# RMSNorm and matmul on one core: without four reads of 12 to 15 rows on the SyncE queue

## Chip, core and metric

The kernel runs on 1 core of one Trainium2 chip. The metric is the device time of one execution in microseconds (us). Engines are named as in the profile: PE is TensorE (matmul), PEld its weight load, DVE is VectorE, ACT is ScalarE, POOL is GpSimd and SP is SyncE, which here only issues DMAs. A name with a q (SPq) is the sequencer of that engine. L191 is line 191 of the kernel.

## What is computed

```python
# x: [16, 1024, 512] float32, gamma: [512], weight: [512, 768], eps = 1e-5
rms = np.sqrt(np.mean(x ** 2, axis=-1, keepdims=True) + eps)
x_norm = x / rms * gamma
return np.matmul(x_norm, weight).astype(np.float32)
```

The 16 x 1024 rows are flattened to 16,384 rows of 512. The output has 16,384 rows of 768.

## The kernel before

**Tiles.** The rows are cut into NT = 128 tiles of 128 rows, and the main loop runs over NP = 64 pairs of tiles; j is the pair. x comes in by groups of 16 tiles (XG), in two buffers `xt`, most groups as two loads of 8 tiles (2 MB each). The output leaves by groups of 8 tiles (OG), in three buffers `ot`: one store of 3 MB for a group, and smaller stores for the first two groups and the last. The last group is stored as two halves of 4 tiles (1.5 MB each).

**Work on a pair.** POOL casts x to bf16 (`cast`, L94; `cast_quad`, L158). For most pairs PE transposes it, two bf16 values taken as one float32 word (`transpose_word`, L133), and DVE copies the result out of PSUM (`evac`, L140). From the second group on, the last two pairs of each group of 16 tiles are transposed by DVE in 32x32 blocks instead (L172). ACT computes the sum of squares (`square`, L98) and the root (L102), and DVE the reciprocal (L104). PE multiplies by the weights (`matmul`, L194), which have been scaled by gamma and cast to bf16 once. `finish_tile` scales the accumulator by 1/rms into `ot`, on ACT (L176) for the first tile of a pair and on DVE (L178) for the second, and calls `store`, which issues a DMA (L191) when the last tile of its stretch is done.

**Order.** The order on each engine is that in which the code is written; there is no scheduler. All loads of x, the weights and all stores are issued on SP, so they stand in one queue there. `load_until` issues the loads ahead of use; the last two are issued in the pass of j = 47. From then on SP issues only stores, and the four reads below. A DMA also waits for the previous user of its completion semaphore; eight of these are used in rotation by the DMAs of SP and ACT.

**The reads.** `probe` is a buffer of 16 partitions and 16 x 64 floats, which nothing reads. `mark` issues for each k in its list one DMA on SP (L265), from the first 4k floats of the first k rows of x, to k partitions of `probe`. `marks` calls it once, at j = NP - 10 = 54, with k = 12, 13, 14, 15. Each of the k rows is a packet of 16k bytes: 192, 208, 224 and 240 bytes.

Of the kernel before, what the change touches and what calls it, by code (L numbers as in the profile page):

```python
# [12 lines left out]
F32 = mybir.dt.float32  # L13
# [5 lines left out]
def kernel(  # L19
# [8 lines left out]
    nc = tc.nc  # L28
    P = 128

    x = x.flatten_outer_dims()
    out = out.flatten_outer_dims()
# [4 lines left out]
    NP = NT // 2  # L37
# [25 lines left out]
    singles = ctx.enter_context(tc.tile_pool(name="singles", bufs=1))  # L63
# [23 lines left out]
    def load_until(i):  # L87
        while starts and starts[0] < i:
            load(starts.pop(0))

    def cast(i, engine, n=1):
        if i // 2 not in xb_tiles:
            xb_tiles[i // 2] = xbp.tile([P, 2, D], BF16, name="xb")
        engine.tensor_copy(out=xb_tiles[i // 2][:, i % 2:i % 2 + n, :], in_=held(x_tiles, XG, i, n))  # L94
# [13 lines left out]
    def norms(i, n):  # L108
        ssq = stats.tile([P, 4], F32, name="ssq")
        for t in range(n):  # L110
            square(i + t, ssq[:, t:t + 1])
        root(i, n, ssq)
# [30 lines left out]
    def transpose_tile(i):  # L143
        for h in range(2):
            transpose_word(i // 2, i % 2, h)
        evac(i // 2, i % 2, 1)
# [6 lines left out]
    def quad_of(j):  # L153
        return j // 2 if (2 * j) % XG >= XG - 4 and 2 * j >= XG else None

    def cast_quad(q):
        quads[q] = quad_in.tile([P, 4, D], BF16, name="xq")
        nc.gpsimd.tensor_copy(out=quads[q], in_=held(x_tiles, XG, 4 * q, 4))  # L158
        turned = quad_out.tile([P, 4, 2, P, 2], BF16, name="xTq")
        for n in range(2):  # L160
            xT_tiles[2 * q + n] = turned[:, 2 * n:2 * n + 2]
        words = quads.pop(q).rearrange("p t d -> p (t d)").bitcast(F32).rearrange("p (a w) -> p a w", w=P)
        out_words = turned.rearrange("p t h m c -> p (t h m c)").bitcast(F32).rearrange("p (a m) -> p a m", m=P)
        for tokens in range(0, P, B):
            for features in range(0, P, B):
                quad_moves.append((out_words[features:features + B, :, tokens:tokens + B],
                                   words[tokens:tokens + B, :, features:features + B]))

    def move_quad(n):
        for _ in range(min(n, len(quad_moves))):  # L170
            dst, src = quad_moves.pop(0)
            nc.vector.transpose(out=dst, in_=src)  # L172

    def scale(engine, dst, src, r):
        if engine is nc.scalar:
            nc.scalar.mul(out=dst, in_=src, mul=r)  # L176
        else:
            nc.vector.tensor_single_scalar(out=dst, in_=src, scalar=r, op=mybir.AluOpType.mult)  # L178

    def accumulator():  # L180
        return opsum.tile([P, 2, WIDE], F32, name="ops").rearrange("p a b -> p (a b)")
# [16 lines left out]
    def matmuls(i, acc, ks, feed=None):  # L198
        for k in ks:
            matmul(i, k, acc, 0, WIDE)  # L200
            if feed:
                feed()
            matmul(i, k, acc, WIDE, O)

    def finish_tile(i, acc, engine):
        scale(engine, out_tile(i), acc[:, :O], rstd_of[i])
        store(i)


    def feeder(pairs, gaps, alone=False):  # L210
        queue = [(j, t, h) for j in pairs for t in range(2) for h in range(2)]
        calls = iter(gaps)

        def feed():
            for _ in range(next(calls)):
                j, t, h = queue.pop(0)
                transpose_word(j, t, h)
                if alone and h == 1:
                    evac(j, t, 1)
                elif (t, h) == (1, 1):  # L220
                    evac(j)
        return feed

    with tc.manual_schedule():
        g_row = singles.tile([2, P, 2], F32)
        nc.scalar.dma_start(out=g_row, in_=gamma.rearrange("(h w c) -> h w c", w=P, c=2))
        nc.scalar.preload_act_table(AF.Sqrt)  # L227
        wv = weight.rearrange("(h w c) o -> w h (c o)", w=P, c=2)
        w_f32 = singles.tile([P, K, O], F32)

        def load_weights(h):
            nc.sync.dma_start(out=w_f32[:, 2 * h:2 * h + 2, :].rearrange("p c o -> p (c o)"), in_=wv[:, h, :])  # L232

        load_until(2)
        load_weights(0)
        load_weights(1)
        load_until(2 * XG)

        for _ in range(20):
            nc.sync.drain()  # L240


        warm = singles.tile([P, WIDE], BF16)
        nc.vector.memset(warm, 0.0)
        eps_sb = singles.tile([P, 1], F32)
        nc.vector.memset(eps_sb, float(eps))  # L246
        ident_f = singles.tile([P, P], F32)
        make_identity(nc, ident_f)
        spare = accumulator()

        def warm_up(n):
            for _ in range(n):
                nc.tensor.matmul(out=spare[:, :WIDE], lhsT=warm[:, :P], rhs=warm, start=True, stop=True)  # L253

        w_bf = singles.tile([P, K, O], BF16)

        def weights(k, engine, lo=0, hi=O):
            scale(engine, w_bf[:, k, lo:hi], w_f32[:, k, lo:hi], g_sb[:, k % 2, k // 2:k // 2 + 1])


        probe = singles.tile([16, 16 * 64], F32)

        def mark(counts):
            for k in counts:
                nc.sync.dma_start(out=probe[:k, 64 * k:64 * k + 4 * k], in_=x[:k, :4 * k])  # L265

        warm_up(6)
        gp = tpsum.tile([P, 2, 2], F32, name="tp")
        for c in range(2):
            nc.tensor.transpose(out=gp[:, c, :], in_=g_row[:, :, c], identity=ident_f[:2, :2])  # L270
        g_sb = singles.tile([P, 2, 2], F32)
        nc.vector.tensor_copy(out=g_sb, in_=gp)  # L272
        cast(0, nc.gpsimd)
        cast(1, nc.gpsimd)
        cast(2, nc.gpsimd, 2)
        norms(0, 2)
        warm_up(4)
        transpose_tile(0)
        transpose_tile(1)
        warm_up(2)  # L280
        weights(0, nc.vector, 0, WIDE)
        weights(0, nc.vector, WIDE, O)
        weights(1, nc.scalar)
        acc = [accumulator() for _ in range(2)]
        for i in range(2):
            matmuls(i, acc[i], [0, 1])
        weights(2, nc.vector)
        weights(3, nc.scalar)
        norms(2, 2)
        cast(4, nc.gpsimd)  # L290
        cast(5, nc.gpsimd)
        matmuls(0, acc[0], [2, 3])
        finish_tile(0, acc[0], nc.scalar)
        matmuls(1, acc[1], [2, 3], feeder([1], [2, 2], alone=True))
        finish_tile(1, acc[1], nc.vector)
        cast(6, nc.gpsimd, 2)

        mid, one, two, both = ([0, 0, 1, 1, 0, 1, 1, 0], [1, 1, 0, 1, 1, 0, 0, 0], [1, 0, 1, 0, 1, 0, 1, 0],
                               [1, 1, 1, 1, 1, 1, 1, 1])
        marks = {NP - 10: (12, 13, 14, 15)}  # L300
        for j in range(1, NP):
            load_until((2 * j + AHEAD + XG - 1) // XG * XG)
            if j + 3 < NP and quad_of(j + 3) is None:
                cast(2 * j + 6, nc.gpsimd, 2)
            if (2 * j + 2) % XG == 0 and 2 * j + 2 < NT:
                cast_quad((2 * j + 2 + XG - 4) // 4)
            elif 2 * j >= XG:
                move_quad(3)
            if j < 4:
                norms(2 * j + 2, 2)  # L310
            if 3 <= j < NP - 2:
                norms_by_four(j + 2)
            if j in marks:
                mark(marks[j])
            if j < 3:
                feed = feeder([j + 1], mid if j == 1 else one, alone=j == 1)
            elif j == 3:
                feed = feeder([4, 5], both)
            elif j + 2 < NP and quad_of(j + 2) is None:
                feed = feeder([j + 2], two)  # L320
            else:
                feed = None
            for i, engine in ((2 * j, nc.scalar), (2 * j + 1, nc.vector)):
                a = accumulator()
                matmuls(i, a, range(K), feed)
                finish_tile(i, a, engine)
# [35 lines left out]
```

## Time and profile before

| what | value |
|---|---|
| median of 6 runs | 210.61 us (210.40 to 210.86) |
| the profiled execution, its own time | 210.46 us |
| its span, first to last instruction | 208.7 us |
| mean granted TensorE clock | 0.979 |
| read from HBM, written to it | 35.14 MB, 50.33 MB |
| mean DMA rate over the span | 411 GB/s |
| busy share of PE, DVE, ACT, POOL | 93%, 72%, 72%, 31% |
| DMA issues | 1 on ACT, 42 on SP |

The issues on SP are 16 loads of x, 2 of the weights, 20 stores and the 4 reads. "Busy" is the time in which an engine works on instructions; issuing and waiting do not count. The DMA share is the mean busy share of the core's 16 DMA engines; 1.00 means that all 16 are at work (single stretches can read slightly above it, since a packet counts where it begins). Landing times come from the semaphore updates that a DMA makes, one for each of the DMA engines that carry a part of it.

### The profile page before, as it was taken

The numbers are of one execution on the slowest core, as the hardware profiler recorded it, in microseconds if no ns is written. First come the engines' busy times: TensorE is split into PE (matmuls) and PEld (weight loads), VectorE is DVE, ScalarE is ACT, GpSimd is POOL, SyncE is SP. The second block draws the span as 40 slices with busy tenths as digits, with TensorE's granted clock in tenths as the row PEclk, the third lists the DMA queues.
The fourth block names the chain that finished last, engine by engine and source line by source line (L and its number), as shares of the span: only waits on it lengthen the run. The fifth ranks groups of instructions, "written<-read, shape, count | busy, mean of one in ns | idle before, by whom it ended". The sixth has DMA issues, their size and how long they took to land.

```text
span 208.7 us, 3478 instructions
## 1 busy us (share of the span) xinstructions
PE 194.3 (93%) x1238; PEld 129.6 (62%) x1238; DVE 150.9 (72%) x270; ACT 149.3 (72%) x358; POOL 64.6 (31%) x65
## 2 busy tenths in 40 slices
PE   7799999999999999999999999999999999999700
PEld 2367767665667666666766667666676667766400
DVE  0465657997399957998499957998499957998300
ACT  4698787778677887788777887788777884986300
POOL 3247535003910292055210562006610365000000
PEclk9999999999999999999999999999999999999965
DMA  6999999999999999999999999999999999999991
GB/s 241 425 440 433 345 409 419 473 422 405 448 438 419 430 410 429 427 443 435 418 418 440 437 429 415 421 438 433 440 421 413 440 435 443 420 396 400 388 415 75
DMA packets 5601, 85.69 MB, mean 411 GB/s; under 512 B 718, under 2 KB 720, under 8 KB 1488
## 3 DMA queue, kind: packets, MB, share of 16 engines
q1 hardware_dynamic: 5580, 85.47, 96.9%
q8 instruction: 9, 0.15, 0.3%
q14 instruction: 8, 0.07, 0.1%
q10 hardware_dynamic: 4, 0.00, 0.0%
HBM read 35.14 MB, written 50.33 MB: 410 GB/s over the span
## 4 chain that ended last, share of the span: by engine, by line
PE 78%; DMA 14%; POOL 1%; DVE 1%; SPq 1%; issue 1%; POOLq 0%
PE ops L194 69%; DMA xt<-in_x_dram 14%; PE tp L133 9%; POOL xb L94 1%; DVE ot L178 1%; SPq L232 0%; SPq L83 0%; SPq L191 0%; POOLq L94 0%; DVE xT L140 0%
## 5 line engine op out<-in xcount | busy, mean ns | idle before, releaser
L194 PE MATMUL ops<-w_bf,xT 128*128 128x512 bf16 (+1 forms) x800 | 147.5, 326 | 0.6 <-DVE w_bf L178 0.6
L194 PEld LDWEIGHTS <-xT 128*128 128x128 bf16 x800 | 78.3, 98 | 46.3 <-issue 0.8
L176 ACT ACTIVATE ot<-ops,rstd 128x768 f32<-128x768 f32 x64 | 57.6, 901 | 41.9 <-PE ops L194 39.5
L94 POOL CAST xb<-xt 128x1024 bf16<-128x1024 f32 (+1 forms) x52 | 51.1, 1010 | 97.6 <-DMA xt<-in_x_dram 86.2
L98 ACT ACTIVATE jk<-xt 128x512 bf16<-128x512 f32 x128 | 78.8, 619 | 1.9 <-DMA xt<-in_x_dram 1.9
L178 DVE TENSOR_SCALAR ot<-ops,rstd 128x768 f32<-128x768 f32 x64 | 64.6, 1010 | 9.5 <-PE ops L194 9.0
L133 PE MATMUL tp<-ident_f,xb 128*128 128x128 f32 x200 | 53.9, 273 | 1.1 <-POOL xb L94 1.1
L140 DVE COPY xT<-tp 128x1024 bf16<-128x1024 bf16 (+1 forms) x53 | 34.7, 656 | 25.3 <-PE tp L133 24.5
L172 DVE STREAM_TRANSPOSE xTq<-xq 32x256 f32<-32x256 f32 x112 | 48.7, 435 | 1.9
L194 PE MATMUL ops<-w_bf,xTq 128*128 128x512 bf16 x224 | 42.8, 326 | 0.0
L133 PEld LDWEIGHTS tp<-ident_f,xb 128*128 128x128 f32 x200 | 28.1, 141 | 4.9 <-POOL xb L94 2.4
L194 PEld LDWEIGHTS <-xTq 128*128 128x128 bf16 x224 | 22.0, 98 | 12.3
L98 ACT ACTIVATION_READ_ACCUMULATOR jk<-xt 128x1 f32 x128 | 24.4, 190 | 0.0
L158 POOL CAST xq<-xt 128x2048 bf16<-128x2048 f32 x7 | 13.3, 1896 | 12.6 <-DMA xt<-in_x_dram 8.8
L102 ACT ACTIVATE rms<-ssq,eps_sb 128x4 f32<-128x4 f32 (+1 forms) x35 | 10.4, 297 | 1.1
L104 DVE RECIPROCAL rstd<-rms 128x4 f32<-128x4 f32 (+1 forms) x35 | 6.1, 175 | 6.1 <-ACT rms L102 5.4
L253 PE MATMUL ops<-warm 128*128 128x512 bf16 x12 | 5.0, 571 | 1.2 <-DVE eps_sb L246 1.2
L253 PEld LDWEIGHTS <-warm 128*128 128x128 bf16 x12 | 1.4, 128 | 2.9 <-issue 1.7
L176 ACT ACTIVATE w_bf<-w_f,g_sb 128x768 bf16<-128x768 f32 x2 | 1.9, 936 | 1.3 <-DMA w_f<-in_weight_dram 1.3
L272 DVE COPY g_sb<-tp 128x4 f32<-128x4 f32 x1 | 0.2, 163 | 3.2 <-PE tp L270 3.2
L227 ACT ACT_TABLE_LOAD x1 | 1.3, 1283 | 1.3 <-PEq L343 1.3
L178 DVE TENSOR_SCALAR w_bf<-w_f,g_sb 128x512 bf16<-128x512 f32 (+2 forms) x3 | 1.4, 482 | 0.5 <-DMA w_f<-in_weight_dram 0.5
(10 smaller groups left out, 1.9 us busy)
## 6 DMA issues: line engine op xcount, KB each, us to landing
out_dram<-ot SPq DMA_DIRECT2D x13, 3072.0 KB, 18.0
xt<-in_x_dram SPq DMA_DIRECT2D x11, 2048.0 KB, 18.3
xt<-in_x_dram SPq DMA_DIRECT2D x2, 4096.0 KB
out_dram<-ot SPq DMA_DIRECT2D x5, 1536.0 KB, 10.9
w_f<-in_weight_dram SPq DMA_DIRECT2D x2, 768.0 KB, 4.9
out_dram<-ot SPq DMA_DIRECT2D x2, 768.0 KB, 17.8
xt<-in_x_dram SPq DMA_DIRECT2D x2, 512.0 KB, 3.4
xt<-in_x_dram SPq DMA_DIRECT2D x1, 1024.0 KB
```

The source lines that it names most:

```text
L94: engine.tensor_copy(out=xb_tiles[i // 2][:, i % 2:i % 2 + n, :], in_=held(x_tiles, XG, i, n))
L98: nc.scalar.activation(out=jk, in_=held(x_tiles, XG, i)[:, 0, :], func=AF.Square, accum_out=ssq)
L102: nc.scalar.activation(out=rms[:, :n], in_=ssq[:, :n], func=AF.Sqrt, scale=1.0 / D, bias=eps_sb)
L104: nc.vector.reciprocal(out=rstd[:, :n], in_=rms[:, :n])
L133: nc.tensor.transpose(out=tp_tiles[j][:, t, h, :], in_=words[:, lo:lo + P], identity=ident_f)
L140: nc.vector.tensor_copy(out=dst[:, t:t + n, :], in_=src[:, t:t + n, :])
L158: nc.gpsimd.tensor_copy(out=quads[q], in_=held(x_tiles, XG, 4 * q, 4))
L172: nc.vector.transpose(out=dst, in_=src)
L176: nc.scalar.mul(out=dst, in_=src, mul=r)
L178: nc.vector.tensor_single_scalar(out=dst, in_=src, scalar=r, op=mybir.AluOpType.mult)
L194: nc.tensor.matmul(out=acc[:, lo:hi], lhsT=xT_tiles[i // 2][:, i % 2, k // 2, :, k % 2], rhs=w_bf[:, k, lo:hi], start=(k == 0), stop=(k == ...
L253: nc.tensor.matmul(out=spare[:, :WIDE], lhsT=warm[:, :P], rhs=warm, start=True, stop=True)
```

## The change

The buffer `probe`, the function `mark`, the dictionary `marks` and the call are removed. Nothing else differs. In the built program SP has 102 instructions in place of 106, and the other engines have the same instructions in the same order. The last four stores use other completion semaphores of the rotation, and the buffers that are allocated behind `probe` may lie elsewhere in SBUF.

```diff
-        probe = singles.tile([16, 16 * 64], F32)
-
-        def mark(counts):
-            for k in counts:
-                nc.sync.dma_start(out=probe[:k, 64 * k:64 * k + 4 * k], in_=x[:k, :4 * k])
...
-        marks = {NP - 10: (12, 13, 14, 15)}
         for j in range(1, NP):
             load_until((2 * j + AHEAD + XG - 1) // XG * XG)
...
-            if j in marks:
-                mark(marks[j])
```

## Prediction

> **What bounds the kernel now.** I read the page first, then the end of the run by stretches, then SP's waits and SP's timeline, then the line of the four reads, and last the trace's records of single packets and semaphore updates around them.
>
> The page, sections 1 and 3 (busy us, share, instructions; then queue, packets, MB, share of 16 engines):
>
> ```profile
> span 208.7 us, 3478 instructions
> ...
> PE 194.3 (93%) x1238; PEld 129.6 (62%) x1238; DVE 150.9 (72%) x270; ACT 149.3 (72%) x358; POOL 64.6 (31%) x65
> ...
> q1 hardware_dynamic: 5580, 85.47, 96.9%
> q8 instruction: 9, 0.15, 0.3%
> q14 instruction: 8, 0.07, 0.1%
> ```
>
> TensorE is busy for 93% of the span, but the 16 DMA engines are busy for 97%. Two things are near their limit, and the end must tell which one sets the time. The end by stretches (us, then busy time and count of each engine, granted clock, DMA share, GB/s):
>
> ```profile
> 160.00:187.00 27.00, 27.00 (x177) 18.37 (x176) 22.72 (x41) 20.71 (x52) 7.92 (x7) 1.00 1.01 433
> 187.00:190.00 3.00, 3.00 (x20) 1.80 (x19) 2.88 (x7) 2.60 (x7) 0.00 (x0) 1.00 0.61 262
> 190.00:197.00 7.00, 7.00 (x45) 4.12 (x42) 3.40 (x5) 3.24 (x6) 0.00 (x0) 1.00 1.00 422
> 197.00:204.30 7.30, 0.18 (x2) 0.00 (x0) 1.02 (x1) 0.00 (x0) 0.00 (x0) 0.71 0.96 407
> 204.30:207.70 3.40, 0.00 (x0) 0.00 (x0) 0.00 (x0) 0.00 (x0) 0.00 (x0) 0.50 0.10 43
> ```
>
> Read the DMA share, second from the right. It is full up to 187, drops to 0.61 for 3 us, is full again, and is 0.10 in the last 3.4 us: about 0.10 x 16, two engines, are at work there alone. TensorE ended at 197. SP's waits from 165 us on (waiter <- releaser: us in total, times, longest):
>
> ```profile
> SPq L191 <- DVE ot L178: 27.4, 4, 12.0
> SPq L357 <- DMA out_dram<-ot: 9.0, 1, 9.0
> ```
>
> The kernel's last wait is SP's, 9.0 us for the last store to land (issued 198.30, landed 207.61). The semaphore updates in the trace show why. A DMA over all 16 engines makes 16 of them, one as each engine's share lands:
>
> ```
> DMA (issued)            first   middle  last three
> store at 152.88        172.83   174.45  175.87 176.86 177.54
> store at 164.92        180.07   181.72  183.14 185.21 185.59
> store at 175.91        187.43   189.02  190.44 192.85 192.87
> store at 188.33        196.93   196.99  198.02 200.09 200.31
> store at 193.10        200.59   200.70  201.69 203.73 203.97
> store at 198.30        204.28   204.39  205.30 207.36 207.61
> ```
>
> Two engines, the laggards, run some 3 us behind the rest at the end. The others run dry around 187 to 190, waiting for the next store; the laggards never do. For them 3072 KB takes 7.3 us (8 packets of 24,576 B at 0.912 us), and the differences of the last column are 7.28, 7.44, 3.66 and 3.64 us: back to back to the end. **So the laggards' total load sets the end from 165 us on**, and TensorE, DVE and SP have some 5 us of slack against it (last store issued 198.30, laggards free for it at 203.97).
>
> **The change part by part.** Without the reads, 4 instructions leave SP's program, 54 small packets leave the DMA queue and one unused buffer leaves SBUF. No instruction on the other engines changes place. SP's timeline there (start us, us to the end of the last one), and the source line of the reads (duration ns min/median/max, first and last start us):
>
> ```profile
> 164.92 0.34 SPq L191 DMA_DIRECT2D out_dram<-ot  x1
> 165.32 4.33 SPq L265 DMA_DIRECT2D probe<-in_x_dram  x4
> 175.91 0.38 SPq L191 DMA_DIRECT2D out_dram<-ot  x1
> ```
>
> ```profile
> L265 SPq DMA_DIRECT2D probe<-in_x_dram x4: 1001/1022/1137, 165.3 to 168.6; - x4
> ```
>
> *SP's issue time.* Four issues take 1.0 to 1.1 us each, 4.33 us from first to last. Behind them on SP's queue stands only the store at 175.91, whose wait for DVE ends at 175.89; SP is done with the reads at 169.65. So 6.2 us of waiting cover it and removing it gains 0. Were that cover gone, the store could be issued 4.33 us earlier, and it still would queue behind work that the engines finish only from 179.7 on.
>
> *The packets.* The reads stand in the queue behind the store of 164.92 and ahead of the one of 175.91. On the engine that reaches them first, packet starts are 179.701 (192 B), 179.719 (208 B), 179.738 (224 B), 179.757 (240 B), and the next store's first packet starts at 179.777: 76 ns for all four, semaphore writes included, or 19 ns each. One engine has only the 224 and 240 B packets, one only the 240 B, one none. The laggards can be told apart: the 12-row read has one late update (185.41, the next latest is 182.25), the 13-row read one, the 14- and 15-row reads two. So one laggard carries four of the packets and the other two: 0.076 and 0.038 us. The last store's two last updates lie 0.25 us apart; the later laggard in the store of 164.92 (185.59) is the one with two packets, since the 12-row read's late update, 185.41, is the other one's 185.21 plus the 0.2 us that lie between updates there. The gain at the end is therefore 0.04 to 0.08 us; I take 0.06.
>
> *Bounds of that price.* The updates of one laggard's four reads lie 0.2 us apart (185.41, 185.62, 185.82, 186.01). If an engine stood still until each landing, four would cost 0.8 us, which is the upper end. The lower end is 0. I take the packet starts, as the following store decides it: its first update comes 7.36 us after the previous store's (187.43 - 180.07), and 8 x 0.912 + 0.076 is 7.37, which leaves nothing for standing still.
>
> The Trainium skill's page "DMA: Bandwidth & Descriptors", section "Latency and other measured facts", puts the least round trip of a tiny HBM transfer at about 0.8 us; four in series would by that be 3.2 us (an estimate), a gain of 1.5%, where the packet starts of this trace show 0.076 us. The same section says that DMA engines 7 and 15 usually are the slower ones; were the deciding one 15, which the reads never touch, the gain would be 0, but here both laggards carry reads.
>
> *Semaphores.* Completion semaphores are used in rotation, eight of them, and a DMA waits for the previous user of its own. Without the reads the last four stores move to other ones. Before, their previous users landed at 164.99, 169.90, 177.54 and 185.59, that is 10.9, 18.4, 15.6 and 12.7 us ahead of the issue. After, these are loads and stores that landed at 140.39, 145.25, 152.58 and 160.11, over 33 us ahead. No wait arises.
>
> *Layout.* Without the unused buffer (4,096 B per partition) tiles behind it in SBUF shift, and SP's program is shorter (106 to 102 instructions), so instruction pages may move. No row shows this alone. The nearest: the q14 instruction packet (8,192 B) takes about 0.31 us of one engine, so one such page off or onto a laggard is 0.3 us less or more; and means of 24,576 B packets over 5 us stretches vary between 913 and 931 ns, 2%. Applied to one laggard's work after the reads (185.6 to 207.6, 22 us) a shift of 1% is 0.2 us, either way. I take 0 and keep 0.3 us both ways.
>
> The sum: profiled span 208.7 - 0.06 = 208.6 us, nothing next in line, since the laggards stay last. The profiled execution took 210.46 us (1.8 us around its span), the median of the six runs is 210.61, so 0.15 more: 210.61 - 0.06 = 210.55 us. A measurement of this kernel can tell about 0.2%, 0.42 us, from no change (the six runs span 210.40 to 210.86); the forecast is no change.
>
> **The rivals.**
>
> *The reads hold the engines longer than their packets show (faster).* Taking the landing distance, 0.8 us goes: 209.8 us. It passes 0.2% from 0.105 us per read on the laggard with four. For it: the updates 0.2 us apart. Against: the 7.36 us above. With a page leaving a laggard, some 210.2, still within 0.2%.
>
> *The writes behind the reads lose their stagger (slower).* The reads delay some engines by 76 ns and others by 38, 19 or 0. Without them the store of 175.91 and all that follows start with other offsets between engines, and if packets then collide more, each takes longer. The place is the laggards' 22 us after the reads; the price, if all took 950 instead of 912 ns (the slowest tenth in 190 to 195 us is at 945), is 4% or 0.9 us: 211.5 us. It decides from 1.9%, 930 ns. For it: means of 926 and 931 ns do occur after 190 us. Against: engines already lie 5.5 us apart there, six packets, so 76 ns makes no order that was not there.
>
> **How the numbers follow.** Forecast, no change within 0.2%: 0.77. Faster by more: 0.12 (0.06 for the reads holding engines, 0.06 for layout in the kernel's favour). Slower by more: 0.11 (0.06 for the lost stagger, 0.05 for layout). The band of no change around 210.61 is 210.19 to 211.03; with a little of the layout cases on both sides the range is 210.1 to 211.05 us.
>
> **What would show it.** Right: SP idle from 165.3 to 175.9; stores issued at the same times within 0.1 us; packets under 512 B down by 108 (54 reads and 54 semaphore writes); the last store issued at 198.3 and landing at about 207.5; DMA share still about 0.10 in the last 3.4 us. Wrong: a gap between landings of the stores of 164.92 and 175.91 that shrinks by over 0.1 us on the laggards (reads held the engine), 24,576 B packets after 180 us at a mean over 930 ns (stagger), or laggards that lie nearer to or farther from the rest already before 165 us (layout). A change in the last store's issue time that moves the end would refute the reading that the laggards' load decides.

## The result and the profile after

The changed kernel takes 210.43 us (median of 37 runs), the kernel before 210.67 us (median of 75 runs beside them). The ratio is 0.9986, with a 95% interval of 0.9980 to 0.9993: 0.29 us faster, between 0.15 and 0.42 us. That is no change by the prediction's bound of 0.2%, and inside its range; but it is a gain clear of zero, and almost five times the 0.06 us of the sum.

The page of the changed kernel, its first lines, the line of packets and the queues:

```profile
span 208.3 us, 3474 instructions
...
PE 194.0 (93%) x1238; PEld 129.3 (62%) x1238; DVE 150.8 (72%) x270; ACT 149.5 (72%) x358; POOL 64.6 (31%) x65
...
DMA packets 5493, 85.68 MB, mean 411 GB/s; under 512 B 610, under 2 KB 612, under 8 KB 1380
...
q1 hardware_dynamic: 5472, 85.46, 97.0%
q8 instruction: 9, 0.15, 0.3%
q14 instruction: 8, 0.07, 0.1%
```

Packets of the queue fall from 5580 to 5472, by the 54 reads and their 54 semaphore writes, and those under 512 B from 718 to 610. The busy times of the engines are those of before within 0.3 us, and the instruction packets are the same. SP's timeline from 160 us on has five stores in one row, and nothing between them:

```profile
165.33 33.72 SPq L191 DMA_DIRECT2D out_dram<-ot  x5
```

The end by the same stretches as before:

```profile
160.00:187.00 27.00, 27.00 (x177) 18.40 (x176) 22.71 (x42) 20.82 (x51) 7.91 (x7) 1.00 1.01 432
187.00:190.00 3.00, 3.00 (x21) 1.83 (x20) 2.91 (x5) 2.60 (x9) 0.00 (x0) 1.00 0.65 279
190.00:197.00 7.00, 7.00 (x45) 4.18 (x43) 3.79 (x7) 3.42 (x7) 0.00 (x0) 1.00 0.99 417
197.00:204.30 7.30, 0.60 (x4) 0.20 (x2) 1.02 (x1) 0.24 (x1) 0.00 (x0) 0.84 0.98 412
204.30:207.70 3.40, 0.00 (x0) 0.00 (x0) 0.00 (x0) 0.00 (x0) 0.00 (x0) 0.50 0.10 43
```

The picture is the same: a dip of the DMA share at 187 to 190, and 0.10 in the last stretch, the work of two late engines (the laggards of the prediction). The fourth row shows one difference. TensorE works 0.60 us beyond 197, against 0.18 before: in this execution it runs 0.42 us later, from long before the place of the reads (the store of 141.49 us before is issued at 141.91). The last store is issued at 198.72 against 198.30, and the kernel ends earlier all the same. That fits the reading that TensorE and the issue of the last store do not set the end.

What does differ is in SP's waits from 165 us on:

```profile
SPq L191 <- DVE ot L178: 43.5, 5, 12.0
SPq L348 <- DMA out_dram<-ot: 8.2, 3, 3.6
```

Before, SP's final wait for stores was one of 9.0 us; now it is three, none over 3.6 us. The wait instructions at the end of SP's program, one line for each kernel (count, ns min/median/max; L357 before is L348 after), say the same:

```profile
L357 SPq EVENT_SEMAPHORE  x7: 17/28/8958, 198.7 to 208.6; - x7
```

```profile
L348 SPq EVENT_SEMAPHORE  x7: 17/28/28, 199.1 to 208.2; - x7
```

Behind the kernel's last DMA SP waits for every completion semaphore in turn, in five instructions (of the seven in these lines) that had the same order in every profile. Their times in the trace (start, end in us, and the DMA whose landing it needs last):

```
before                                        after
198.677  207.635  last store (207.613)        199.098  199.126  -
207.672  207.700  -                           200.111  200.139  store at 188.75 (200.094)
207.733  207.761  -                           203.763  203.791  store at 193.52 (203.746)
207.798  207.826  -                           207.419  207.447  last store (207.402)
207.859  207.886  -                           207.481  207.509  -
208.677  end of the span                      208.293  end of the span
```

Before, the last store's semaphore belongs to the first of the five, so the four others start only after the landing, about 0.062 us apart. With four DMAs fewer, the last store takes a semaphore four places away in the rotation of eight, and that one belongs to the fourth wait: three waits have been done by then. From the last landing to the end of the span it is 208.677 - 207.613 = 1.064 us before and 208.293 - 207.402 = 0.891 us after. **0.173 us of the gain lie behind the last landing.** With the 0.06 us of packets the sum is 0.23 us.

The two profiles' last landings also differ by 0.21 us, more than the packets explain. That is not to be read: the next section's profiles show that it moves by as much from one execution to the next.

### The profile page after: what moved, and what is told of

It reads as the page before. It is cut to its first block, busy times and chain, and to the rows that moved or that the text cites. A ratio compares the mean times of both kernels' runs of the same rounds, so it can differ in the third digit from the quotient of the medians.

```text
span 208.3 us, 3474 instructions
## 1 busy us (share of the span) xinstructions
PE 194.0 (93%) x1238; PEld 129.3 (62%) x1238; DVE 150.8 (72%) x270; ACT 149.5 (72%) x358; POOL 64.6 (31%) x65
## 3 DMA queue, kind: packets, MB, share of 16 engines
q1 hardware_dynamic: 5472, 85.46, 97.0%
## 4 chain that ended last, share of the span: by engine, by line
PE 78%; DMA 14%; POOL 1%; DVE 1%; SPq 1%; issue 1%; POOLq 0%
PE ops L194 69%; DMA xt<-in_x_dram 14%; PE tp L133 9%; POOL xb L94 1%; DVE ot L178 1%; SPq L232 0%; SPq L83 0%; SPq L191 0%; POOLq L94 0%; DVE xT L140 0%
## 5 line engine op out<-in xcount | busy, mean ns | idle before, releaser
L253 PE MATMUL ops<-warm 128*128 128x512 bf16 x12 | 4.4, 505 | 1.2 <-DVE eps_sb L246 1.2
```

## Experiments

Theory W: the late engines' packets (0.04 to 0.08 us) and the place of the last store's semaphore among the end waits (0.17 us). Rival P: the reads held the late engines for the whole gain. Rival L: the layout in SBUF. For each profile the time from the last landing to the end of the span was worked out from the trace as above; it is called the tail here. Timed kernels are compared with the kernel before on the same chip. A late engine is one whose update comes some 2 to 3 us behind those of most others in the same store.

**Four reads of one row.** They leave the rotation as it was, and take the packets off the late engines.

```diff
-                nc.sync.dma_start(out=probe[:k, 64 * k:64 * k + 4 * k], in_=x[:k, :4 * k])
+                nc.sync.dma_start(out=probe[:1, 64 * k:64 * k + 4], in_=x[k:k + 1, :4])
```

> The four reads stay, but each takes one row of 16 bytes, so that they load one DMA engine alone. Theory W (the end waits): the last store keeps the completion semaphore that it had before the change, SP's last waits stand in the same order, and the span ends 1.06 us after the last landing as before; only the 0.04 to 0.08 us of packets on the two late engines go: ratio to the kernel before 0.9997 (0.06 us). Rival P (the removed packets held the late engines for all of the 0.24 to 0.29 us that the change brought): the late engines carry no read here either, so the ratio is that of the change, 0.9986, with the last landing 0.2 us earlier and the rest after it as before. Rival L (the layout in SBUF): the buffer is still there, ratio 1.000.

> The four one-row reads once more, on the same chip as the single one: theory W has it 0.23 us (0.11%) slower than the single read, with 1.06 us after the last landing; rival P and the layout have the two alike.

Ratio 0.9994 [0.9982, 1.0005] (210.57 us) on one chip, and 0.9994 [0.9984, 1.0005] (210.50 us) on another. Tail 1.064 and 1.065 us, as in the kernel before. The middle is nearer to W's 0.9997 than to P's 0.9986, but the intervals reach both, so the times alone decide nothing. The profile does for the tail: 0.17 us of the change's gain is absent here, with the reads off the late engines (their updates come at 180.28 to 180.89 us, the late ones of the store ahead at 185.22 and after). The last landings are 207.94 and 207.67 us, later than before's 207.61, which shows how much a landing varies between executions.

**Where the late engines are.**

```diff
-        marks = {NP - 10: (12, 13, 14, 15)}
+        marks = {NP - 10: (5, 6, 8, 10)}
```

> Four reads of 5, 6, 8 and 10 rows with packets of 80 to 160 bytes. The landing records of the reads tell how many of their engines are late: a late last update appears from the read on that reaches the earlier late engine (it is among the first twelve). Expected of the time: that of the kernel before within 0.1 us, since the late engines carry at most 3 small packets, and 1.06 us from the last landing to the end of the span.

The first read, of 5 rows, already has one late update (185.39 us; the next is 182.00), at the time of the last updates of the store ahead (185.16 and 185.19). So in that execution a late engine is among the first five. It carries all four reads, one more packet than the three that were expected at most. Time 210.52 us, tail 1.064 us. This is one execution.

**Does their load set the end?** The reads at their old place, with rows of 8,192 bytes; once with 12 to 15 rows, once with four times 4 rows.

```diff
-        probe = singles.tile([16, 16 * 64], F32)
+        probe = singles.tile([64, 2 * 2048], F32)
+        xw = x.rearrange("(p t) d -> p (t d)", t=4)
...
-            for k in counts:
-                nc.sync.dma_start(out=probe[:k, 64 * k:64 * k + 4 * k], in_=x[:k, :4 * k])
+            for n, k in enumerate(counts):
+                nc.sync.dma_start(out=probe[32 * (n % 2):32 * (n % 2) + k, 2048 * (n // 2):2048 * (n // 2 + 1)], in_=xw[:k, :])
...
-        marks = {NP - 10: (12, 13, 14, 15)}
+        marks = {NP - 10: (4, 4, 4, 4)}      # in the second kernel alone
```

> The four reads of 12, 13, 14 and 15 rows stay where they are, but each row is a packet of 8,192 bytes (about 0.305 us at the rate of the other packets). The reading that the load of the two late engines sets the end: one late engine carries four such packets, 1.22 us in place of 0.076, the other two, 0.61 in place of 0.038; the end comes 0.9 to 1.15 us later, ratio 1.0045 to 1.0055. Against it, the reading that TensorE or the issue of the last store sets the end: ratio 1.000.

> Four reads of 4 rows each, a packet of 8,192 bytes per row: 1.22 us of each of four engines. If the late engines' load sets the end and the earlier one of them is not among these four, the others have about 3 us to spare and the time does not grow: ratio 0.9997, the same as with four one-row reads. If every engine's load counts, ratio 1.005. If the earlier late engine is among the four, ratio about 1.005 too, and the reads' landing records will say so.

12 to 15 rows: ratio 1.0066 [1.0046, 1.0086], 1.4 us slower (1.0 to 1.8). 4 rows: ratio 0.9998 [0.9989, 1.0007]. The same four packets of 8,192 bytes per engine cost 1.4 us where they reach the late engines and nothing that can be measured where they do not. The sum of the bytes does not explain this: the 4-row reads move 131 KB, which at 430 GB/s would be 0.30 us for all engines together, and the interval of their kernel ends at 0.15 us. The last stretch of each, taken up to 210 us, the 12 to 15 rows first:

```profile
204.30:210.00 5.70, 0.00 (x0) 0.00 (x0) 0.00 (x0) 0.00 (x0) 0.00 (x0) 0.50 0.19 80
```

```profile
204.30:210.00 5.70, 0.00 (x0) 0.00 (x0) 0.00 (x0) 0.00 (x0) 0.00 (x0) 0.50 0.11 45
```

The tails are 1.059 and 1.065 us, so all of it is ahead of the last landing (209.63 and 207.80 us). In the profile of the first, the latest engine's updates of the four reads lie at 186.38, 186.70, 187.01 and 187.32, after 186.10 for the store ahead: 1.22 us for four packets, as worked out beforehand. From there it needs 22.3 us to the end; before it needed 22.0 from 185.59, its small packets included. The other 0.5 us by which this profile's last landing is later was there ahead of the reads (186.10 against 185.59). The middle of the measured loss lies above the expected 0.9 to 1.15 us by some 0.25 us, within the interval; what this would be is open. In this profile both of the two latest engines take part in the 12-row read, and in the kernel before only one. So which engines are late is not the same in every profile. The record does not name the chip of the kernel before's profile, so whether this goes by chip or by execution is open.

**How many end waits stand behind the last landing.** One, two and three one-row reads move the last store's semaphore through the other places.

```diff
-        marks = {NP - 10: (12, 13, 14, 15)}
+        marks = {NP - 10: (15,)}             # one; two: (14, 15); three: (13, 14, 15)
```

with the one-row line of the first experiment.

> One read of one row (16 bytes) in place of four, so that the last store gets the semaphore that SP waits for in the last of its five end waits. Theory W (the end waits, 0.062 us each): 0.83 us from the last landing to the end of the span, against 1.06 in the kernel before and 0.89 in the changed one; with the packets off the late engines ratio 0.9986 to the kernel before, 0.23 + 0.06 us. Rival P (only the packets count): 1.06 us after the last landing, or a ratio like that of four one-row reads.

> Two one-row reads: the last store has the semaphore of the third of the five end waits, so two waits come behind it. Theory W: 0.83 + 2 x 0.062 = 0.95 us from the last landing to the end of the span. Rival P: a constant, whatever the semaphore.

> Three one-row reads: the second of the five end waits, three waits behind it. Theory W: 0.83 + 3 x 0.062 = 1.02 us from the last landing to the end of the span (the kernel before, with four behind it: 1.06). Rival P: a constant.

The tail in all profiles in which the stores are the kernel before's:

```
reads late in the run   end wait of the last store   tail, us
four                    1st of 5                      1.064 1.064 1.065 1.064 1.065 1.059
three                   2nd                           1.000
two                     3rd                           0.939
one                     5th                           0.829 0.830
none (the change)       4th                           0.891 0.896
```

The size of the reads and the time of the last landing do not matter to it, the place does: 0.05 to 0.06 us a place. This shows the term of W that lies behind the landing, and P's constant is refuted. Ratios: the single read 0.9981 [0.9970, 0.9991] (210.31 us, 0.19 us below the four one-row reads on the same chip, where 0.23 was expected; their runs overlap). Two and three reads had one run each, 210.41 and 210.19 us, too few to say more than the tail does.

**The change and the single read side by side.**

> The changed kernel once more, beside the single read on the same chip. Theory W (the end waits): 0.89 us after the last landing, ratio 0.9989 to the kernel before (0.17 us of end waits and 0.06 of packets), and 0.06 us slower than the single read. Rival P: the same ratio, but with the difference in the last landing and not behind it.

> The single one-row read again. Theory W: 0.83 us after the last landing, ratio 0.9986. Rival P: as the changed kernel, with the same time after the last landing.

0.9983 [0.9973, 0.9993] and 0.9984 [0.9976, 0.9993]; 210.38 and 210.37 us against 210.75. Both are faster than the kernel before; from each other they can't be told by time. The single read ends 0.066 us sooner after the last landing, which is not enough to call it better. Its buffer is back in SBUF and it is as fast, which leaves no room for a layout effect of the size that rival L needs.

Of the seven ratios with an interval for which W names a number (that of the change and those of the two kernels here, both kernels with four one-row reads, the first single read and the 4-row reads), six lie below it, by 0.0002 to 0.0006, or 0.04 to 0.13 us; W's number is inside each interval. So a further gain of about 0.1 us, beside the end waits and the 0.06 us of packets, is neither shown nor excluded.

**An attempt at the late engines.** In the store before the last one, 16 of the 128 partitions were given to other engines.

```diff
-            nc.sync.dma_start(out=rows(out, first, n), in_=held(o_tiles, OG, first, n))
+            dst, src = rows(out, first, n), held(o_tiles, OG, first, n)
+            if i != NT - 5:
+                nc.sync.dma_start(out=dst, in_=src)
+            else:
+                nc.sync.dma_start(out=dst[:112], in_=src[:112])
+                for p in range(112, P, 4):
+                    nc.sync.dma_start(out=dst[p:p + 4], in_=src[p:p + 4])
```

> The changed kernel, with the store before the last one cut in pieces: 112 partitions as one DMA over 16 engines, the other 16 partitions as four DMAs of 4, which run on four engines that are not late. The late engines carry 7 packets of 12,288 bytes in place of 8, 0.46 us less; the four others carry 3 more each, 1.4 us, of the 3 us that they have to spare. Four DMAs more put the last store back on the kernel before's semaphore, 1.06 us from the last landing to the end. If the late engines' load sets the end: 0.46 + 0.06 us faster than the kernel before, ratio 0.9975. If the total DMA work or the issue of the last store sets it: ratio 1.000 or above.

> The same relief, and five one-row reads at the old place, so that the last store has the semaphore of the last end wait: 0.83 us after the last landing. Theory W: 0.23 us faster than the relief alone, 0.75 us faster than the kernel before, ratio 0.9964. Rival P: as the relief alone, 0.9975.

The second of these has the diff above and one-row reads with `(11, 12, 13, 14, 15)` at the old place.

Both missed: 1.0086 [1.0061, 1.0110] and 1.0064 [1.0048, 1.0080], slower by 1.8 and 1.3 us. The tails are 1.064 and 0.829 us, as the semaphores have it. The loss is ahead of the last landing (209.29 and 209.86 us). The windows of the first of the two, and then of the single read, whose stores are uncut (the last two columns are DMA share and GB/s):

```profile
197.00:199.00 2.00, 0.00 (x0) 0.00 (x0) 1.00 (x1) 0.00 (x0) 0.00 (x0) 1.00 1.00 344
199.00:201.00 2.00, 0.00 (x0) 0.00 (x0) 0.00 (x0) 0.00 (x0) 0.00 (x0) 0.92 0.87 270
201.00:203.00 2.00, 0.00 (x0) 0.00 (x0) 0.00 (x0) 0.00 (x0) 0.00 (x0) 0.50 0.73 270
```

```profile
197.00:199.00 2.00, 0.00 (x0) 0.00 (x0) 1.02 (x1) 0.00 (x0) 0.00 (x0) 1.00 1.00 424
199.00:201.00 2.00, 0.00 (x0) 0.00 (x0) 0.00 (x0) 0.00 (x0) 0.00 (x0) 1.00 0.94 399
201.00:203.00 2.00, 0.00 (x0) 0.00 (x0) 0.00 (x0) 0.00 (x0) 0.00 (x0) 0.69 1.03 436
```

The engines are as busy from 197 to 199 and move 344 in place of 424 GB/s: some of the packets became longer. Packets of 12,288 bytes between 195 and 202 us take 582 ns on average, against 464; the median is 460 in both within 1 ns, and 35 of 115 take over 500 ns, against none. One long packet of another size makes up most of the loss in both profiles: the last to end of the 3072 KB store ahead takes 2.25 us where 0.91 is usual, and that store lands at 201.63 and 201.80 us in place of 200.31 before. SP also needs longer, 1.07 to 2.01 us for each piece and 2.01 and 1.49 us for the last store; but the latest engine is free for that store only at 205.03 and 205.04 us, so this is not what it waits for. Moving the work was tied to another shape of transfer, and that shape cost more than the 0.46 us it was to save. So this is no test of the late engines' reading, and whether the 112-partition cut or the pieces of four partitions lengthen packets was not separated.

## Why the prediction was right, and what it missed

*What sets the end*: right. The last stretch is again the work of about two engines; a store issued 0.42 us later does not delay the end; load on the late engines counts fully and load on four others not measurably. That the late engines are always the same two, as the text took for granted, was wrong: in the kernel before one of them is in all four reads and the other in two, in the profile with the rows of 8,192 bytes both are in all four. The row on DMA engines 7 and 15 that the prediction quotes calls its best guess at a cause specific to SWDGE, that is, to descriptors made by software; the queue that carries this kernel's data is named `hardware_dynamic` in the profile, so the row gives no reason to look for these two here.

*SP's issue time*: right, nothing came of it. The prediction had stores issued within 0.1 us of before; they came 0.42 us later, but already ahead of the reads' place.

*The packets*: the estimate of 0.04 to 0.08 us is not contradicted, and not shown either. Taken in order of time, the last two updates of the store behind the reads come 7.64 and 7.27 us after those of the store ahead of them in the profile of before, and 7.62 and 7.22 us in that of the changed kernel: 0.01 and 0.05 us less, in unrounded times. The nine other profiles in which no read reaches the late engines and no row has 8,192 bytes have 7.57 to 7.62 and 7.24 to 7.27; the kernel before lies only 0.01 us above these. With reads of 5 to 10 rows, where one late engine carries four small packets, it is 7.62 and 7.22 again. The first updates of the two stores show the price better: they lie 7.36 us apart before, and 7.23 to 7.28 in the ten profiles without the small packets there, where the four packets were put at 0.076. The price as such was tested on the 8,192-byte rows, where 1.22 us were worked out and 1.0 to 1.8 measured; for rows of 192 to 240 bytes it is too small for a time to show.

*Semaphores*: this step failed. It followed the rotation to the waits ahead of each store's issue, rightly found them long satisfied, and concluded that no wait arises. It did not follow it to the other place where the same semaphores are waited for, SP's last five instructions. The sentence that nothing is next in line behind the last landing hid 1.06 us there, of which up to 0.23 us depends on which semaphore the last store holds, and 0.17 us went with this change. This missing term is three times the one that was worked out, and the two together, 0.23 us, agree with the measured 0.29 [0.15, 0.42]. So the forecast of no change held by luck in part: it put this term at nothing without having looked for it, and the term happens to be smaller than the 0.42 us up to which a gain counted as no change.

*The rivals.* Reads that hold the engines longer: not seen; these gaps shrank by 0.05 us at most, under the 0.1 named as the sign. Loss of stagger: not seen; packets of 24,576 bytes between 180 and 195 us take 919.9 ns on average before and 918.5 after. Layout: not seen; the last two updates of the store ahead of 165 us are at 176.86 and 177.54 before, 176.85 and 177.41 after, and the single read has the buffer and the gain.

## What to carry to other kernels

Follow a completion semaphore to every instruction that waits for it, the waits at the program's end too: adding or removing DMAs ahead of the last store turns the rotation, and with it the place of the last store in a serial list of end waits. Ask of each transfer not how many bytes it has but which DMA engines carry it, and whether those are the ones that finish last. An effect of 0.1% that times can hardly separate can be exact in the trace, if it is measured between two events that both lie behind the noise.

## What the runs showed that was not expected

- The end waits: 0.05 to 0.06 us for each place, 0.23 us from the first place to the last, steady to 0.01 us over fourteen profiles, while the last landing itself varies from 207.40 to 207.94 us with the stores uncut and the reads small.
- With a store of 112 partitions and four stores of 4 partitions behind it, packets of the same size take 582 ns on average in place of 464, and even the 3072 KB store ahead of them in the queue lands at 201.63 us in place of 200.31.
- SP needs 1.00 to 1.14 us to issue a read of 12 to 15 rows, 0.75 to 0.83 us for one of as many rows of 8,192 bytes, 0.74 to 1.12 us for one of a single row, and 0.33 to 0.38 us for a store of 128 partitions, which moves about a thousand times the bytes of the reads of 12 to 15 rows. Only behind the cut store did a store of 128 partitions take longer, 1.49 and 2.01 us.
